# A gated attention and convolution block: first products stored unscaled, a second buffer for the attention's values, the gate pool opened after the attention

## The chip, the core and the metric

One core of a Trainium2 chip runs the whole layer in one launch. The metric is device microseconds of an execution; the median of three runs of the kernel before is 1504.21 us (1502.57 to 1506.20). The profiled execution took 1508.27 us, with a span of 1506.5 us from its first to its last instruction. Engines: PE multiplies matrices (PEld loads its weights), DVE and ACT work element by element, POOL and SP here mostly issue transfers (DMA). Each engine runs its own instructions in order and waits on semaphores of the others.

## The reference

x is 2048 tokens by 1024 in float32. Cut to what matters:

```python
h = rmsnorm(x, norm_g)
q, k, v, z_att, gb, gc, u, z_conv, g_att, g_conv = split(h @ w_in)       # 1024 x 6144
att = chunked_rel_attention(q, k, v, rel_bias)      # 8 heads of 64; own chunk of 64 and 8 to the left
y_att = (att * silu(z_att)) @ w_att_out
vconv = causal_depthwise_conv(gc * u, conv_w, conv_b)
y_conv = (gb * vconv * silu(z_conv)) @ w_conv_out
m = sigmoid(g_att) * y_att + sigmoid(g_conv) * y_conv
out = rmsnorm(x + m @ w_out, final_norm_g)
```

rmsnorm multiplies each token by r = 1/sqrt(mean(x^2) + eps), so that a product of unscaled x can be multiplied by r afterwards. The sigmoids are computed as 0.5 (1 + tanh(0.5 g)).

## The kernel before

**Precision and tiles.** Every large product is made of three fp32r passes: each operand is split into a high part (an ACT cast) and a low part (a DVE subtraction), and `passes` (L137) issues high x high, high x low and low x high for each of four blocks of 128, that is 12 matmuls of 128x128 by 128x512. The input projection works on tokens in two halves of 1024 and on weight columns in 24 pairs of two blocks of 128. For each pair and half it makes seven products instead of eight, numbered 1, 2, 6, 7, 4, 5, 3 (`ORDER`), of sums and differences of quarters: the operands of x are called t1 to t7 (`operand_steps`, each four tiles: t10h, t10l, t11h ...), those of the weights wc (`operand`, L377), which are also stored to HBM in the first half and loaded from there in the second. `seq` lists all products (pair, number) in order; before product s the weights of product s + 3 are made.

**The first products.** The first three pairs (`PLAIN`) of the first half are gate columns. They are done as twelve direct products of 24 matmuls each, on unscaled x, in the order (pair, 512 tokens, block) of `plain` (L642), while r (tiles rb, one for each 512 tokens) is worked out beside them. Each of the first four is copied out of PSUM by ACT and scaled later; of the others DVE reads PSUM itself and multiplies by rb (`scaled`, L652). Then ACT takes the Tanh and issues the store of the gate (`ev_gate`, L413). `between` builds t1, t2, t6, t7, t4 from the sixth product on. Products use three PSUM banks in turn (`ps_d`). In this stretch the order on PE, DVE and ACT is that of the code; elsewhere a scheduler orders all engines by its own estimate.

**Seam of the halves.** While the last pair of the first half runs, t1 to t7 of the second half are built, one set each time the list `due` says so (L849: two products after each of that pair's seven). The last pairs' results (silu of z, tiles sz; v) are evacuated at the same time.

**The attention** (`attention`, L145) runs between the products of the second half, spread evenly over them: 32 steps of (512 queries, head), four units each, and the values product (`att_v`, L229) three units behind. Its loads are issued by POOL: `load_qk` one head ahead, into two buffers, and `load_v` for the present head, into one buffer vv.

**The output stage.** For each half, `half_c` takes 16 items (branch i, 128 columns d) of two products each: wy times mid, then DVE combines with the gate tiles gl and so evacuates PSUM (L960, L963). Gates come from HBM through a pool gp of five tiles, which is opened some pairs before the attention ends (L867); `make_c` loads weights and gates one item ahead. `mix` prepares the operands of `half_d`, the last projection with the residual and the final norm.

Tiles named e(...) come from a pool of eight, used in turn, and slot(...) from one of 56. SP issues most of the other transfers, in one queue.

## Time and profile before

| what | us |
|---|---|
| median of three runs | 1504.21 |
| profiled execution / its span | 1508.27 / 1506.5 |
| PE busy / DVE / ACT / POOL | 1475.3 / 1090.5 / 740.1 / 163.8 |
| mean granted clock of PE | 0.995 |
| first products, from the first matmul on x | 8.3 to about 85.5 |
| second half begins | about 499 |
| output stage begins | 1172.0 |

In a row of the order of time the first number is the start in us, the second the length, and the bracket holds the idle time of that engine before it and what ended it. A row of the list of waits gives the total, the number and the longest. In the table of stretches each engine has its busy time and its number of instructions, and the three numbers at the end are the granted clock of PE (1.00 is full), the mean share of the DMA engines and the rate in GB/s. DMA is idle in much of the first products and near full from 90 us on.

### The profile page before, as it was taken

The page shows a single profiled execution, that of the slowest core. Times are in us where ns is not written, and L with a number is a line of the kernel's source. Part 1 is how long each engine was busy: PE and PEld are TensorE (multiplying, and loading weights), DVE is VectorE, ACT ScalarE, POOL GpSimd, SP SyncE. Part 2 cuts the span into 40 slices and gives each one's busy share as a digit, 9 for nine tenths or more (in the row PEclk, how much of TensorE's full clock was granted, in tenths as well). Part 3 has the DMA queues.
Part 4 walks back from the last instruction along what each step waited for, and adds up shares of the span by engine and source line. Part 5 has one row for each costly group of instructions (what it writes and reads, how often), then busy time and mean ns, then how long its engine had stood idle before and what let it go on. Part 6 is the DMA issues. An engine that isn't in the chain of part 4 may idle for free. (4 is left out here: it accounts for less than half of the span.)

```text
span 1506.5 us, 21077 instructions
## 1 busy us (share of the span) xinstructions
PE 1475.3 (98%) x6976; PEld 1226.2 (81%) x6976; DVE 1090.5 (72%) x2121; ACT 740.1 (49%) x1399; POOL 163.8 (11%) x310
## 2 busy tenths in 40 slices
PE   8899999999999999999999999999999999999997
PEld 6778888888877788887888888888888888888886
DVE  7977588596557784676677777787765577767687
ACT  7363453444345333565566666666666223423153
POOL 0000000000000002232222323322220000010000
PEclk9999999999999999999999999999999999999999
DMA  5279899989988895999898887878989845877443
GB/s 214 73 273 352 308 361 351 348 295 328 345 304 287 314 341 173 339 341 337 288 295 286 259 260 249 265 256 264 310 282 314 307 129 168 294 262 240 153 162 112
DMA packets 168748, 408.28 MB, mean 271 GB/s; under 512 B 21056, under 2 KB 41536, under 8 KB 168640
## 3 DMA queue, kind: packets, MB, share of 16 engines
q1 hardware_dynamic: 137008, 316.48, 60.7%
q0 software_dynamic: 22272, 73.42, 15.4%
q10 hardware_dynamic: 9360, 17.04, 3.1%
q8 instruction: 55, 0.90, 0.2%
q14 instruction: 53, 0.43, 0.1%
HBM read 251.67 MB, written 155.19 MB: 270 GB/s over the span
## 5 line engine op out<-in xcount | busy, mean ns | idle before, releaser
L162 POOL DMA_DIRECT2D q<-q x128 | 66.8, 527 | 675.5 <-DVE wc L128 585.0
L204 ACT ACTIVATE pr<-ps_s,nmax 128x640 f32<-128x640 f32 (+4 forms) x128 | 93.5, 730 | 93.0 <-DVE nmax L200 92.3
L206 ACT ACTIVATE pr<-pr,rs 128x640 f32<-128x640 f32 (+4 forms) x128 | 97.9, 765 | 35.3 <-DVE rs L205 34.9
L200 DVE CUSTOM_DVE_ANT_0 ps_s<-ps_s,bs 128x640 f32<-128x640 f32 (+4 forms) x128 | 95.3, 744 | 23.7 <-PE ps_s L194 22.4
L140 PE MATMUL ps_d<-mid,wy 128*128 128x512 f32 x256 | 99.7, 389 | 0.8 <-ACT wy L127 0.8
L128 DVE TENSOR_TENSOR wc<-wraw,wc 128x512 fp32r<-128x512 f32 x120 | 82.3, 688 | 24.7 <-ACT wc L127 24.5
L141 PE MATMUL ps_d<-mid,wy 128*128 128x512 f32 x256 | 99.6, 389 | 0.0
L194 PE MATMUL ps_s<-kk,q 128*128 128x320 f32 (+1 forms) x448 | 98.5, 334 | 1.0 <-ACT pr L204 0.5
L142 PE MATMUL ps_d<-mid,wy 128*128 128x512 f32 x256 | 99.3, 389 | 0.0
L220 DVE TENSOR_TENSOR pt<-ps_t,pt 128x640 fp32r<-128x640 f32 (+4 forms) x128 | 94.1, 735 | 3.4 <-ACT pt L219 2.5
L127 ACT CAST wc<-wraw 128x512 fp32r<-128x512 f32 x120 | 74.1, 621 | 44.2 <-PE ps_c L142 23.0
L219 ACT CAST pt<-ps_t 128x640 fp32r<-128x640 f32 (+4 forms) x128 | 80.1, 626 | 21.9 <-PE ps_t L214 20.7
L214 PE MATMUL ps_t<-ident,pr 128*128 128x128 f32 x560 | 82.3, 273 | 0.2
L229 PE MATMUL po<-pt,vv 128*128 128x512 f32 x336 | 75.5, 356 | 4.1 <-DMA vv<-v 3.2
L229 PEld LDWEIGHTS po<-pt,vv 128*128 128x128 f32 x336 | 62.1, 188 | 19.1 <-issue 3.5
L214 PEld LDWEIGHTS ps_t<-ident,pr 128*128 128x128 f32 x560 | 65.7, 140 | 9.9 <-issue 1.5
L194 PEld LDWEIGHTS ps_s<-kk,q 128*128 128x128 f32 x448 | 67.6, 190 | 5.6 <-ACT pr L204 4.8
L997 PE MATMUL ps_w<-wo,lefth 128*128 128x512 f32 (+1 forms) x240 | 71.9, 382 | 0.0
L140 PEld LDWEIGHTS ps_d<-mid,wy 128*128 128x128 f32 x256 | 48.0, 188 | 11.1 <-ACT wy L127 1.2
L234 DVE TENSOR_TENSOR ot<-po,ot 64x256 f32<-64x256 f32 x64 | 26.6, 415 | 41.3 <-ACT ot L233 40.4
L141 PEld LDWEIGHTS ps_d<-mid,wy 128*128 128x128 f32 x256 | 48.0, 188 | 10.1
L142 PEld LDWEIGHTS ps_d<-mid,wy 128*128 128x128 f32 x256 | 48.1, 188 | 9.9
(535 smaller groups left out, 4110.4 us busy)
## 6 DMA issues: line engine op xcount, KB each, us to landing
wc<-wc SPq DMA_DIRECT2D x294, 512.0 KB, 5.3
wraw<-wp_in SPq DMA_DIRECT2D x54, 512.0 KB, 5.8
q<-q POOLq DMA_DIRECT2D x128, 128.0 KB, 5.0
gl<-gate SPq DMA_DIRECT2D x64, 256.0 KB, 2.8
mid<-mid SPq DMA_DIRECT2D x64, 256.0 KB, 5.3
wor<-wo SPq DMA_DIRECT2D x56, 256.0 KB, 5.2
bs<-bias POOLq DMA_DIRECT2D x32, 320.0 KB, 7.7
v<-vst SPq DMA_DIRECT2D x64, 128.0 KB, 4.6
```

The costliest lines, as they stand in the source:

```text
L128: nc.vector.tensor_sub(w[:, 1], src, w[:, 0].bitcast(F32))
L140: nc.tensor.matmul(ps, lhsT=w[:, 0, k, :], rhs=rh[:, cs], start=(first and not onto and k == 0), stop=False, skip_group_check=onto)
L141: nc.tensor.matmul(ps, lhsT=w[:, 0, k, :], rhs=rl[:, cs], start=False, stop=False, skip_group_check=onto)
L142: nc.tensor.matmul(ps, lhsT=w[:, 1, k, :], rhs=rh[:, cs], start=False, stop=(last and k == len(rhs) - 1), skip_group_check=onto)
L194: nc.tensor.matmul(ps[:, i, :m], lhsT=q[s][:, g * P:(g + 1) * P], rhs=kk[:, k1 - n + i * m:k1 - n + (i + 1) * m], start=(s == 0), stop=(s ...
L200: nc.vector.tensor_tensor_reduce(out=view, in0=view, in1=bv, scale=-0.125, scalar=3.0e38, op0=ALU.add, op1=ALU.min, accum_out=nmax)
L204: nc.scalar.activation(out, view, AF.Exp, bias=nmax, scale=-1.0, accum_out=rs)
L206: nc.scalar.activation(pr[:, :n], pr[:, :n], AF.Identity, scale=rs)
L214: nc.tensor.transpose(out=ps[:, j * P:(j + 1) * P], in_=pr[:, j * P:(j + 1) * P], identity=ident)
L219: nc.scalar.copy(hi[:, js, qs], src)
L220: nc.vector.tensor_sub(lo[:, js, qs], src, hi[:, js, qs].bitcast(F32))
L229: nc.tensor.matmul(ps[:, :, a * P:b * P], lhsT=vv[:, g0 + j, :], rhs=pt[:, j, :, a * P:b * P], start=(i == 0), stop=(i == len(js) - 1))
```

## The change

- The twelve first products are all copied out of PSUM by ACT and stored as they are by SP (`plain_d`); the two rb tiles are stored too. `scaled` and the deferred Tanh are gone from this stage.
- In the output stage's first half the gates of the three unscaled columns are loaded, multiplied by rb (loaded again as `rbs`) on DVE and put through Tanh on ACT. The items' order begins with columns 3 and 7, which have no such gates, and `mix` follows it.
- vv gets two buffers and is loaded one head ahead, with q and k; the load of z stays where it was.
- gp is opened only when the attention is over; the first item's gates go into tiles of the pool of eight.
- The sets t1 to t7 of the second half are built at products 2, 3, 5, 8, 12, 15, 17 counted from the last pair's first (before: 2, 3, 4, 6, 8, 10, 12).

```diff
+TURN = (2, 3, 5, 8, 12, 15, 17)
...
+    plain_d = [dram.tile([P, CH], F32, name=f"plain{q}") for q in range(4 * PLAIN)]
+    rb_d = [dram.tile([P, CH], F32, name=f"rb{c}") for c in range(2)]
...
         def load_v(c, h):
-            vv = at([P, 8, P], "vv")
+            vv = at([P, 8, P], "vv", bufs=2)
...
+
+        def load_z(c, h):
             if h % 2 == 0:
...
         load_qk(*todo[0])
+        load_v(*todo[0])
...
                     load_qk(*todo[i // 4 + 1])
+                    load_v(*todo[i // 4 + 1])
                 elif i % 4 == 2:
-                    load_v(*todo[i // 4])
+                    load_z(*todo[i // 4])
...
-    def gate(i, d, c):
-        g = gp.tile([P, CH], F32, tag="g", name="gl")
-        nc.sync.dma_start(g, gate_d[i][d][c])
+    def gate(i, d, c, make):
+        g = make("gl")
+        nc.sync.dma_start(g, plain_d[plain.index((d, i, c))] if unscaled(d, c) else gate_d[i][d][c])
         return g
 
-    ITEMS_C = [(i, d) for dd in ((0, 4, 1, 5), (2, 6, 3, 7)) for i in (1, 0) for d in dd]
+    def unscaled(d, c):
+        return d < PLAIN and c < 2
+
+    ITEMS_C = [(i, d) for dd in ((3, 7, 0, 4), (1, 5, 2, 6)) for i in (1, 0) for d in dd]
...
-    def scaled(p, n, c, src):
-        t = src if src.space != PSUM else e("c")
-        nc.vector.tensor_mul(t, src, rb[c])
-        late.append(lambda: evs[p][n](c, c, t))
...
                 rb[0] = inverse(ry[0], e)
+                store(rb_d[0], rb[0])
...
-            if q < 4:
-                t = e("plain")
-                nc.scalar.copy(t, ps)
-                copied.append(lambda p=p, n=n, c=c, t=t: scaled(p, n, c, t))
-            else:
-                now, late = late, []
-                between(q)
-                if q > 4:
-                    scaled(*held0)
-                held0 = (p, n, c, ps)
-                for fn in now:
-                    fn()
+            t = e("plain")
+            nc.scalar.copy(t, ps)
+            store(plain_d[q], t)
+            between(q)
...
-            due.append(s + 2)
+                due = [s + d for d in TURN]
...
-        if n == NPAIR + 2 + PLAIN + 16 and i == 1:
-            conv_stack.close()
-            gp = pool("gp", 5)
         if n == 2 * NPAIR - 1 and i == 5:
-            made = make_c(0, ITEMS_C[0])
+            made = make_c(0, ITEMS_C[0], e)
+            rbs = [fslot("rbs") for c in range(2)]
+            for c in range(2):
+                nc.sync.dma_start(rbs[c], rb_d[c])
...
     banks.close()
+    conv_stack.close()
+    gp = pool("gp", 5)
...
+            if d < PLAIN and not hf:
+                for c in cs:
+                    nc.vector.tensor_mul(gl[c], gl[c], rbs[c])
+                    nc.scalar.activation(gl[c], gl[c], AF.Tanh, scale=0.5)
...
-                mix((7, 10, 14, 15).index(n_))
+                mix((3, 0, 1, 2)[(7, 10, 14, 15).index(n_)])
```

How the instructions move, at three places. First ACT among the first products, from the last cast of t6 on (c and plain are results on their way to a gate, wc the first weights of the seven-product part). Before:

```order
L133 CAST t63h<-xs 128x512
L416 ACTIVATE plain<-plain 128x512
L417 DMA gate_0_1_156<-plain 128x512
L416 ACTIVATE plain<-plain 128x512
L417 DMA gate_0_1_188<-plain 128x512
L416 ACTIVATE c<-c 128x512
L417 DMA gate_1_1_160<-c 128x512
L133 CAST t70h<-xs 128x512
L133 CAST t71h<-xs 128x512
L133 CAST t72h<-xs 128x512
L133 CAST t73h<-xs 128x512
L416 ACTIVATE c<-c 128x512
```

Now:

```order
L136 CAST t63h<-xs 128x512
L721 COPY plain<-ps_p 128x512
L136 CAST t70h<-xs 128x512
L136 CAST t71h<-xs 128x512
L136 CAST t72h<-xs 128x512
L136 CAST t73h<-xs 128x512
L721 COPY plain<-ps_p 128x512
L136 CAST t40h<-xs 128x512
L136 CAST t41h<-xs 128x512
L136 CAST t42h<-xs 128x512
L136 CAST t43h<-xs 128x512
L130 CAST wc<-wraw 128x512 x2
```

The Tanh and the gate's issue are gone, a copy out of PSUM stands between the sets, and the first wc is twelve rows behind t63h. Second, DVE at the seam of the halves (sz are silu values that SP stores as z, v and u results on their way, t71l to t50l splits for the second half). Before:

```order
L468 SCALAR_TENSOR_TENSOR sz<-sz,v 128x512
L134 TENSOR_TENSOR t40l<-xs,t40h 128x512
L358 TENSOR_TENSOR xs<-xs 128x512
L134 TENSOR_TENSOR t41l<-xs,t41h 128x512
L358 TENSOR_TENSOR xs<-xs 128x512
L134 TENSOR_TENSOR t42l<-xs,t42h 128x512
L815 TENSOR_TENSOR v<-v,ps_c 128x512
L134 TENSOR_TENSOR t43l<-xs,t43h 128x512
L362 TENSOR_TENSOR t_4851<-xs 128x512
L468 SCALAR_TENSOR_TENSOR sz<-sz,v 128x512
L468 SCALAR_TENSOR_TENSOR sz<-sz,ps_c 128x512
L134 TENSOR_TENSOR t50l<-t_4851,t50h 128x512
```

Now:

```order
L475 SCALAR_TENSOR_TENSOR sz<-sz,v 128x512
L137 TENSOR_TENSOR t72l<-xs,t72h 128x512
L809 TENSOR_TENSOR v<-v,ps_c 128x512
L137 TENSOR_TENSOR t73l<-xs,t73h 128x512
L365 TENSOR_TENSOR xs<-xs 128x512
L475 SCALAR_TENSOR_TENSOR sz<-sz,v 128x512
L475 SCALAR_TENSOR_TENSOR sz<-sz,ps_c 128x512 x2
L137 TENSOR_TENSOR t40l<-xs,t40h 128x512
L365 TENSOR_TENSOR xs<-xs 128x512
L137 TENSOR_TENSOR t41l<-xs,t41h 128x512
L137 TENSOR_TENSOR t42l<-xs,t42h 128x512
L137 TENSOR_TENSOR t43l<-xs,t43h 128x512
```

All sz now stand ahead of t40l; t5 follows further on. Third, POOL at the attention's second head. Before:

```order
L166 DMA kk<-k_0_109 128x512
L169 DMA bs<-bias_476 128x640
L177 DMA vv<-v_0_123 128x512
L182 DMA zs<-z_0_139 128x512
L162 DMA q_5884<-q_0_0_83 64x512 x2
L162 DMA q_5885<-q_1_0_87 64x512 x2
L166 DMA kk<-k_0_111 128x512
L169 DMA bs<-bias_477 128x640
L177 DMA vv<-v_0_125 128x512
```

Now:

```order
L169 DMA kk<-k_0_109 128x512
L172 DMA bs<-bias_490 128x640
L180 DMA vv<-v_0_125 128x512
L187 DMA zs<-z_0_139 128x512
L165 DMA q_5886<-q_0_0_83 64x512 x2
L165 DMA q_5887<-q_1_0_87 64x512 x2
L169 DMA kk<-k_0_111 128x512
L172 DMA bs<-bias_491 128x640
L180 DMA vv<-v_0_127 128x512
```

The values of head n + 1 (v_0_125 is the second head's) stand where those of head n stood. PE's own order differs by the place of one matmul on t20l, near 90 us, and of one in the output stage.

## The prediction

> **What bounds the kernel now.** I read the page's first part, then the waits of PE (the matmul engine), then the granted clock in short windows, and last the order of time on the engines around each wait.

> ```profile
> PE 1475.3 (98%) x6976; PEld 1226.2 (81%) x6976; DVE 1090.5 (72%) x2121; ACT 740.1 (49%) x1399; POOL 163.8 (11%) x310
> ```
> PE is busy for 1475.3 of 1506.5 us, so TensorE bounds the kernel and the change, which leaves the matmuls alone, can only win PE's idle time (31 us with the start and the end) and time at a lowered clock. The list of PE's waits (engine, line, releaser: total us, times, longest) says where:

> ```profile
> PE ps_p L140 <- DVE c L654: 4.7, 2, 2.9
> PE ps_c L140 <- ACT wc L127: 4.4, 2, 3.2
> PE po L229 <- DMA vv<-v: 3.2, 2, 1.8
> PE ps_d L140 <- ACT t33h L133: 1.8, 1, 1.8
> PE ps_d L140 <- ACT wc L127: 1.1, 1, 1.1
> PE ps_d L140 <- DMA wc<-wc: 0.9, 1, 0.9
> PE po L229 <- DVE w L825: 0.8, 1, 0.8
> PE ps_d L140 <- ACT wy L127: 0.8, 1, 0.8
> ```
> In order of time on PE, start and length first, the wait in brackets:

> ```profile
> 22.29 0.40 PE L141 MATMUL ps_p<-rawl,w 128*128 128x512 f32 x1
> 32.73 0.39 PE L142 MATMUL ps_p<-rawh,w 128*128 128x512 f32 x1
> 58.66 0.66 PE L140 MATMUL ps_p<-rawh,w 128*128 128x512 f32 x1 [1.86 <-DVE c L654]
> 74.27 0.50 PE L140 MATMUL ps_p<-rawh,w 128*128 128x512 f32 x1 [2.87 <-DVE c L654]
> 88.65 0.50 PE L140 MATMUL ps_c<-t10h,wc 128*128 128x512 f32 x1 [3.16 <-ACT wc L127]
> 720.03 0.59 PE L229 MATMUL po<-pt,vv 128*128 128x512 f32 x2 [1.84 <-DMA vv<-v]
> 1159.32 1.39 PE L229 MATMUL po<-pt,vv 128*128 128x512 f32 x6 [0.82 <-DVE w L825]
> ```
> The granted clock (PE busy, clock, DMA share and rate; two-us windows):

> ```profile
> 58.00:60.00 2.00, 1.34 (x4) 0.70 0.00 0
> 60.00:62.00 2.00, 2.00 (x6) 0.50 0.94 256
> 74.00:76.00 2.00, 1.73 (x8) 1.00 0.69 259
> 90.00:92.00 2.00, 2.00 (x6) 0.50 1.05 178
> ```
> and, with all engines in five-us windows, around the wait at 720:

> ```profile
> 720.00:725.00 5.00, 4.97 (x18) 4.26 (x19) 2.47 (x6) 2.05 (x5) 0.00 (x0) 0.66 0.97 333
> ```
> A wait of 1.84 us was followed by a window at 0.66, which is 5 x 0.34 = 1.7 us more; the wait before 58.66 by 0.6 + 1.0 = 1.6 us; the longer one before 74.27 by nothing.

> **Part 1, the first products.** The twelve plain products keep their matmuls. What goes is each product's multiplication by rb (L654, DVE), its Tanh and its store on ACT; what comes is one ACT copy each (four had one) and a store on SP, and PSUM is freed by that copy. The end of this stage is set by ACT and DVE, which must split the operands t1, t2, t6, t7, t4 before ACT reaches the first wc:

> ```profile
> 65.77 0.62 ACT L133 CAST t60h<-xs 128x512 fp32r<-128x512 f32 x1 [5.05 <-DVE xs L356]
> 72.27 0.62 ACT L133 CAST t63h<-xs 128x512 fp32r<-128x512 f32 x1 [1.90 <-DVE xs L356]
> 75.88 0.62 ACT L133 CAST t70h<-xs 128x512 fp32r<-128x512 f32 x1 [0.40 <-ACT c L416]
> 80.32 0.62 ACT L133 CAST t40h<-xs 128x512 fp32r<-128x512 f32 x1 [1.73 <-DVE xs L358]
> 86.44 0.62 ACT L133 CAST t43h<-xs 128x512 fp32r<-128x512 f32 x1 [1.42 <-DVE xs L358]
> 87.98 1.14 ACT L127 CAST wc<-wraw 128x512 fp32r<-128x512 f32 x2 [0.40 <-ACT c L416]
> ```
> I redo this chain in the new order on ACT. Two casts start 1.14 - 0.62 = 0.52 us apart. The two PE rows at 22.29 and 32.73 are 46 matmuls apart: 0.227 us each, 5.45 us for a product of 24. On DVE, seven L654 multiplications (some 0.6 us each, counted in its order) ahead of t6 are gone, 4.2 us, so ACT is what is late. (1) t60h now stands behind the copy of the ninth product. That product needs no DVE any more: it starts at 58.66 - 1.86 = 56.80 and ends at 62.25, the copy takes 0.52, t60h comes at 62.8 for 65.77. (2) t60h to t63h is the same add, cast, subtract chain, 6.5 us; I add 0.5, because in it stands an add on weights whose fetch now starts later (SP sends it behind the eighth store): t63h at 69.8. (3) Between t63h and t70h stood three Tanh with their issues, 3.61 us; now cast and copy, 1.04: t70h at 70.8. (4) From t70h to t40h 4.44 us, less one L654: 3.8, t40h at 74.6. (5) t40h to t43h unchanged, 6.12: 80.7. (6) A Tanh and its issue stood before wc; now it is 0.52 behind: 81.2, and the matmul follows 0.67 after the cast as now (87.98 to 88.65): 81.9. **Gain: 88.65 - 81.9 = 6.8 us.** The product phase itself ends at 56.80 + 4 x 5.45 = 78.6, so a wait of some 3.3 us stays, with its spell at clock 0.50 as at 90. The low clock after 58.66 goes too, but wins nothing of its own, as PE was waiting anyway. Bounds: 88.65 - 78.6 = 10.0 above; nothing below, where the stream behind eats it (rival A). Behind SP's twelve stores are the wraw, x and wc transfers, in the order they had; each store waits only for a copy that PE's next step needs anyway.

> **Part 2, the values.** POOL's queue (issue times, what it waited for):

> ```profile
> 696.59 0.55 POOL L177 DMA_DIRECT2D vv<-v  x1 [9.29 <-PE ps_t L214]
> 711.39 0.55 POOL L177 DMA_DIRECT2D vv<-v  x1 [2.05 <-PE ps_t L214]
> 1151.03 0.55 POOL L175 DMA_DIRECT2D vv<-v  x1 [8.95 <-PE po L229]
> ```
> The single buffer comes free when the last head's product is done, and the matmul at 720.03 waited 8.6 us behind the issue. The row at 1159.32 names DVE w, but comes 8.3 us behind its issue in the same way; I count it as the same wait. With two buffers the queue waits at the same places, for the head before, but what it fetches there is needed one head later, about 15 us (696.59 to 711.39). All three waits go: 3.2 + 0.8 = 4.0, and with them the low clock at 720, 1.7. **Gain: 5.7 us.** Bounds 3.2 (only what DMA is named for) and 6.5 (1159 with a low clock as well). Behind the waiting fetch stand z and the next q, k and bias, which waited behind it before too.
> [...]

> **Part 3, the seam of the halves.** TURN builds t6, t7, t4, t5 and t3 of the second half 1, 2, 4, 5 and 5 products later. DVE has no gap there, and SP's queue stands behind it:

> ```profile
> 497.67 0.44 SPq L383 DMA_DIRECT2D wc<-wc  x1
> 502.68 0.32 SPq L474 DMA_DIRECT2D z<-sz  x1
> 505.02 0.62 SPq L383 DMA_DIRECT2D wc<-wc  x1
> ```
> The last z values come out of DVE here, start first:

> ```profile
> 502.56 0.69 DVE L468 SCALAR_TENSOR_TENSOR sz<-sz,ps_c 128x512 f32<-128x512 f32 x1
> 506.16 0.69 DVE L468 SCALAR_TENSOR_TENSOR sz<-sz,ps_c 128x512 f32<-128x512 f32 x1
> ```
> Each z store holds up the wc loads behind it, and PE waits 0.9 and 1.8 us (wc, and the one put down to t33h). In the new order of DVE the last sz stands eleven instructions earlier: 6.6 us at 0.6. The load at 505.02 can go some 4 us earlier, more than the 1.8. **Gain: 2.7 us**, bounds 0 (another row of that queue holds it) and 3.2 (with the 0.5 us wait on v). The moved splits are still six products, 16 us, ahead of use. The two waits of 1.1 and 1.2 us on wc (4.4 in the list, less the 3.2 at 88) are outside it and stay.

> **Part 4, the output stage.** It gets 12 multiplications (0.6 us) on DVE, 12 Tanh (0.5) on ACT, and gates that are fetched only when the attention is over. Cover:

> ```profile
> gl<-gate SPq DMA_DIRECT2D x64, 256.0 KB, 2.8
> 1175.00:1200.00 25.00, 25.00 (x112) 20.71 (x111) 12.48 (x20) 4.58 (x8) 0.00 (x0) 1.00 0.89 302
> 1200.00:1225.00 25.00, 25.00 (x112) 20.67 (x112) 20.54 (x34) 7.38 (x13) 0.00 (x0) 1.00 0.65 206
> ```
> DVE has 17 us free in these 50, ACT 38. A gate takes 2.8 us to land and about 1.3 to scale, 4.1 together; an item is two products, 5.45 us, and its gates are asked for an item ahead. With three PSUM banks an evacuation may come 5 us late before PE waits. I take 0; bounds +0.8 (the wait on wy at the stage's start goes) and -7 (rival B).

> **Sum.** 6.8 + 5.7 + 2.7 = 15.2 us. The profiled execution took 1508.27, which lies 4.1 above the median of the runs, 1504.21; it would take 1493.1. From the median: **1489.0 us**.

> **Rivals.** *A: the stage behind the first products takes the gain back.* The DMA engines run full there from 90 us (share 1.05 above), x of the second half and the stores of wc in one stream:

> ```profile
> 114.74 0.69 DVE L392 TENSOR_TENSOR s<-wraw 128x512 f32<-128x512 f32 x1 [1.75 <-DMA wraw<-wp_in]
> 128.66 0.69 DVE L392 TENSOR_TENSOR s<-wraw 128x512 f32<-128x512 f32 x1 [3.19 <-DMA wraw<-wp_in]
> ```
> If these waits grow by what the start is earlier, and reach PE, 6.8 us are lost: 1495.8. Against it: the bytes come in the same order, only earlier, and PE never waited there. *B: the first gates come late.* In the new order DVE scales item 2's gates ahead of item 1's evacuation; if they land later than an evacuation can slip, PE waits up to an item, 5.45, plus 1.7 of low clock: 1496.2. *C: slower.* Every scaled item (six in the first half of this stage) waits for its whole chain of 4.1 us, because five buffers are too few to fetch ahead: 24.6 us, 1513.6. It decides from 15.2 / 6 = 2.5 us an item. Against it: each buffer is free again at least an item and a half before its next use. *D: the change doesn't do what it says,* all three waits having a second cause just behind: 1504. *E: the low clock stays.* The 1.84 us before 720.03 did not lower the clock, something else in the windows before did, and 1.7 us at 0.66 remain somewhere in the attention: 1490.7. Against it: the wait of 1.86 us before 58.66 was followed by the same.

> **How the numbers follow.** Forecast 0.57 (its own range 1485 to 1493), A 0.15, B 0.12, C 0.05, D 0.06, E 0.05. The range goes down to 1484.5 (the upper bounds of parts 1 and 2 in part) and up past A and B to 1499.5. A difference under 0.2%, 3 us, can't be told from none here. Forecast, A, B and E are beyond it: 0.89, of which I keep 0.87, since A and B could come together; within it D and that, 0.08; slower C, 0.05.

> **What would show it.** First matmul on wc at 81 to 83 us for 88.65, no wait on ps_p; no wait on vv, no low clock near 720; none over 1 us around 500; PE full from the output stage's start. I am wrong if PE waits on wc between 85 and 130, or on gl's evacuation after the attention.

## The result, and the profile after

The change makes the kernel faster by about 8 us, where 15 were forecast. Beside each other on one chip the kernel before had a median of 1504.37 us (1502.57 to 1506.20) and the changed one of 1496.14 us (1494.30 to 1498.76). The ratio is 0.9945 with a 95% interval of 0.9929 to 0.9961, which is 5.9 to 10.7 us. The profiled execution of the change took 1497.31 us (span 1495.5), 11.0 us less than the profiled one of before.

PE is busy for the same share of the span as before, and the list of its waits (engine, line, releaser: total us, times, longest) is of another make:

```profile
PE 1472.5 (98%) x6976; PEld 1223.9 (82%) x6976; DVE 1090.9 (73%) x2121; ACT 746.2 (50%) x1407; POOL 163.8 (11%) x310
```

```profile
PE ps_c L143 <- ACT wc L130: 3.8, 2, 2.5
...
PE po L234 <- DVE pt L225: 1.6, 2, 0.8
PE ps_d L143 <- DMA wc<-wc: 1.4, 1, 1.4
...
PE ps_d L143 <- ACT wc L130: 1.1, 1, 1.1
PE ps_t L219 <- DVE pt L225: 1.0, 2, 0.8
PE ps_s L199 <- ACT pr L209: 0.9, 1, 0.9
PE ps_d L143 <- ACT wy L130: 0.8, 1, 0.8
...
PE ps_d L143 <- ACT gl L945: 0.3, 1, 0.3
```

The waits of ps_p on DVE and the waits on vv and on t33h are gone. Those on pt and pr are 3.5 us together, where the list before had only 0.5 us on pr. In order of time on PE:

```profile
81.27 0.50 PE L143 MATMUL ps_c<-t10h,wc 128*128 128x512 f32 x1 [2.52 <-ACT wc L130]
...
668.48 1.10 PE L234 MATMUL po<-pt,vv 128*128 128x512 f32 x4 [0.80 <-DVE pt L225]
698.84 1.08 PE L234 MATMUL po<-pt,vv 128*128 128x512 f32 x4 [0.76 <-DVE pt L225]
951.70 0.77 PE L219 MATMUL ps_t<-ident,pr 128*128 128x128 f32 x5 [0.79 <-DVE pt L225]
953.41 1.03 PE L199 MATMUL ps_s<-kk,q 128*128 128x320 f32 x4 [0.95 <-ACT pr L209]
```

Both executions have the same 6976 matmuls in nearly the same order, so their starts can be set against each other, the first with the first and so on. The start in the changed kernel less the start before gives a running account of where the time went (each column is rounded by itself):

| place in the program | after minus before, us | this step |
|---|---|---|
| first matmul on wc (88.65, now 81.27) | -7.4 | -7.4 |
| some four us later (low clock there before, none now) | -9.0 | -1.6 |
| before the seam of the halves (484 us) | -9.0 | 0 |
| behind the seam (511, now 499 us) | -11.4 | -2.4 |
| attention, behind the old waits on vv and their low clock (725 us before) | -14.7 | -3.4 |
| attention, at 958 us now | -11.6 | +3.1 |
| end of the attention (1148 us now) | -12.2 | -0.6 |
| first gates of the output stage (1205 us now) | -11.1 | +1.1 |
| end | -11.0 | +0.1 |

The row with +3.1 is the loss that the prediction did not have: 1.6 of it comes by 954 us, most of that from the waits at 951 to 953 (1.7 us, where the kernel before has 0.5), and 1.5 from a spell at half clock behind them (3.41 us from 953.9). This is DVE there, start and length first, the idle time before it and its releaser in brackets:

```profile
950.50 0.41 DVE L240 TENSOR_TENSOR o<-po,ot 64x256 f32<-64x256 f32 x1 [2.61 <-DMA mid<-o]
950.84 0.81 DVE L225 TENSOR_TENSOR pt<-ps_t,pt 128x640 fp32r<-128x640 f32 x1
```

and POOL, which issued that store:

```profile
945.43 0.57 POOL L248 DMA_DIRECT2D mid<-o  x1
```

o is the attention's result of a pair of heads, and has one buffer. DVE may not write the next pair's first result into it before the store of the last pair has been read out of it, 4.5 us after the issue at 946.0. Behind this instruction in DVE's order stands the low part of pt, and PE waits for that. Over the whole attention, the group of these instructions:

```profile
L240 DVE TENSOR_TENSOR o<-po,ot x64: 403/417/420, 604.8 to 1157.4; 64x256 f32<-64x256 f32 x64
...
  DMA mid<-o: 8.8, 5
```

DVE sat 8.8 us at five such places, 4.4 in the kernel before. At the place of the +3.1 the kernel before has the same wait. There its store was read out 3.2 us after the issue, and PE waited 0.5 us behind it:

```profile
960.00 0.56 POOL L243 DMA_DIRECT2D mid<-o  x1
963.72 0.42 DVE L235 TENSOR_TENSOR o<-po,ot 64x256 f32<-64x256 f32 x1 [1.11 <-DMA mid<-o]
```

### The profile page after: what moved, and what is told of

The parts are those of the page before. It is cut to its first block, busy times and chain, and to the rows that moved or that the text cites. A ratio compares the mean times of both kernels' runs of the same rounds, so it can differ in the third digit from the quotient of the medians.

```text
span 1495.5 us, 21091 instructions
## 1 busy us (share of the span) xinstructions
PE 1472.5 (98%) x6976; PEld 1223.9 (82%) x6976; DVE 1090.9 (73%) x2121; ACT 746.2 (50%) x1407; POOL 163.8 (11%) x310
## 5 line engine op out<-in xcount | busy, mean ns | idle before, releaser
L899 ACT ACTIVATE wo<-wor 128x512 fp32r<-128x512 f32 x56 | 34.5, 629 | 60.1 <-DMA wor<-wo 53.1
L143 PEld LDWEIGHTS ps_d<-mid,wy 128*128 128x128 f32 x256 | 48.0, 188 | 12.2 <-ACT wy L130 1.5
## 6 DMA issues: line engine op xcount, KB each, us to landing
mid<-mid SPq DMA_DIRECT2D x64, 256.0 KB, 5.6
wor<-wo SPq DMA_DIRECT2D x56, 256.0 KB, 5.0
gl<-gate SPq DMA_DIRECT2D x52, 256.0 KB, 3.1
```

What stands on the lines that cost most here:

```text
L143: nc.tensor.matmul(ps, lhsT=w[:, 0, k, :], rhs=rh[:, cs], start=(first and not onto and k == 0), stop=False, skip_group_check=onto)
```

## The experiments

The kernels were run in three groups on three chips. In each group the kernel before was timed beside them: its medians were 1506.35, 1506.33 and 1504.73 us, so across groups the ratios to it are compared. The last column is the profiled execution's span.

| run | median us | ratio to before, 95% | span us |
|---|---|---|---|
| scaled first products (part 1 undone) | 1503.35 | 0.9989 (0.9977 to 1.0002) | 1499.5 |
| one values buffer (part 2 undone) | 1498.44 | 0.9954 (0.9942 to 0.9967) | 1495.5 |
| old turn (part 3 undone) | 1497.13 | 0.9950 (0.9933 to 0.9967) | 1493.4 |
| two buffers for o | 1495.57 | 0.9937 (0.9924 to 0.9949) | 1493.1 |
| the change again | 1499.26 | 0.9953 (0.9934 to 0.9971) | 1497.0 |
| two buffers for o, spaced | 1494.56 | 0.9917 (0.9901 to 0.9934) | 1491.4 |
| and sums first | 1487.57 | 0.9873 (0.9853 to 0.9893) | 1485.9 |
| no scaling in the output stage | 1495.59 | 0.9927 (0.9907 to 0.9946) | 1493.1 |
| kernel before, again | 1504.58 | one run | 1502.8 |
| sums first, one values buffer | 1490.99 | 0.9917 (0.9902 to 0.9932) | 1488.5 |
| sums first, old turn | 1491.51 | 0.9911 (0.9899 to 0.9924) | 1488.4 |
| sums first, other space | 1491.22 | one run | 1489.5 |

**Part 1 undone.** The first products are as in the kernel before, and the output stage scales nothing; all else is the change.

```diff
-            t = e("plain")
-            nc.scalar.copy(t, ps)
-            store(plain_d[q], t)
-            between(q)
+            if q < 4:
+                t = e("plain")
+                nc.scalar.copy(t, ps)
+                copied.append(lambda p=p, n=n, c=c, t=t: scaled(p, n, c, t))
+            else:
+                now, late = late, []
...
```

> The changed kernel with part 1 alone undone: the first twelve products are scaled, sent through Tanh and stored as finished gates at once, as before; the output stage scales nothing. Theory (the sum of three parts): PE's first matmul on wc goes back from 81.3 to 88.6 us and a half-clock spell of 3.41 us follows its wait, 7.4 + 1.6 = 9.0 us lost; the output stage wins back the 1.2 us it lost; 1496.1 + 7.8 = 1503.9. Rival (the stage behind the first products holds PE anyway): at most 3 us are lost, 1499.

The two late matmuls come back to the hundredth of a us:

```profile
74.26 0.50 PE L141 MATMUL ps_p<-rawh,w 128*128 128x512 f32 x1 [4.37 <-DVE c L662]
88.65 0.50 PE L141 MATMUL ps_c<-t10h,wc 128*128 128x512 f32 x1 [1.64 <-ACT wc L128]
```

Against the profile of the change the run is 7.4 us behind from here to 668 us, so the stage behind the first products takes nothing back, and the rival falls. A half-clock spell came behind the first of the two waits (matmuls 0.43 us apart from 75.15 to 78.14 us, 0.23 from 78.47 on), where PE had to wait again anyway, and none behind the second, so 7.4 and not 9.0 were lost here. At the end only 4.1 us are left: 1.7 us of the waits on pt (668 and 699 us) do not come in this execution, others behind o cost 0.8 more, no spell at half clock follows them (1.5), and 0.9 is won where the output stage no longer scales. The median is 4.1 us above that of the change run again (1499.26), with nearly equal medians of the kernel before; by the ratios, 0.9989 against 0.9945 and 0.9953, part 1 is worth 5.4 to 6.6 us.

**Part 2 undone.**

```diff
-            vv = at([P, 8, P], "vv", bufs=2)
+            vv = at([P, 8, P], "vv")
...
-                    load_v(*todo[i // 4 + 1])
                 elif i % 4 == 2:
+                    load_v(*todo[i // 4])
                     load_z(*todo[i // 4])
```

> The changed kernel with part 2 alone undone: one buffer for the values, loaded at its own head. Theory (a new wait took most of the gain: DVE waits to overwrite o until the store of o has landed, and PE waits for DVE's pt): the waits on vv come back (two of 1.4 to 1.8 us and the one of 0.8 at 1159), the waits on pt at 668, 699 and 951 get shorter, and the net loss is 1 to 2 us: 1497 to 1498. Rival (the buffer alone was worth what was forecast): 5.7 us lost, 1501.8.

The ratio, 0.9954, is that of the change, 0.9945 and 0.9953. The waits on vv did not come back either, except for one of 0.84 us on po at 677 us, put down to a DVE instruction, and DVE waited 6.0 us for the store of o where it had waited 8.8. The longest wait of this run in the attention is a third thing, on DVE and then on PE:

```profile
1134.85 1.36 DVE L943 TENSOR_TENSOR gl<-gl,rbs 128x512 f32<-128x512 f32 x2 [3.52 <-DMA rbs<-rb]
```

```profile
1137.74 1.65 PE L234 MATMUL po<-pt,vv 128*128 128x512 f32 x6 [2.24 <-DVE pt L225]
```

The scheduler put the first multiplication of a gate by rbs, part 4 of the change, into DVE's order before the attention was over, and its transfer had not landed. In the change itself the same multiplication stands behind the attention, at 1170 us. Between 1100 and 1148 us this run loses 4.1 us on the change for it, a spell at half clock included. So it can't price the buffer: with a cost that the change doesn't have it is as fast as the change. What it does show is that one buffer alone need not bring 4 us of waits on vv.

**Part 3 undone.**

```diff
-TURN = (2, 3, 5, 8, 12, 15, 17)
+TURN = (2, 3, 4, 6, 8, 10, 12)
```

> The changed kernel with part 3 alone undone: the operands of the second half are built at products 2, 3, 4, 6, 8, 10, 12. Theory: waits of 0.9 us on wc and of 1.8 us on t33h come back around 500 us, the 1.4 us on wc that the changed kernel has there goes: 1 to 2.4 us lost, 1497.3 to 1498.5. Rival (the seam's gain came from the earlier start, not from the order): the time stays at 1496.1.

The profile shows the loss where it was expected, the medians do not. The wait on t33h is there:

```profile
PE ps_d L143 <- ACT t33h L136: 2.7, 1, 2.7
```

From 484 to 504 us the run loses 2.4 us on the change, in three steps of 0.6, 0.5 and 1.3. The name t33h is a coincidence of times. The matmul reads t20h and wc, and it starts at 503.60 us, 0.13 us after a wc load has landed; in the kernel before it starts at 510.84, again 0.13 us after a wc load, and in that kernel's second profile (below) it starts ahead of the cast of t33h, 0.14 us after the load. So this is a wait on a wc load, as the prediction had it. Between 660 and 958 us the run gains 5.0: its waits on pt and pr are 2.9 us shorter, and no half clock follows them. So neither theory is settled by this run; the waits behind o had to go first.

**Two buffers for o.** To make room for the second one, two scratch vectors went from three buffers to one; this frees 128 bytes of SBUF per partition.

```diff
-        a = small.tile([P, n], F32, name="ra", tag="ra")
-        q = small.tile([P, n], F32, name="rq", tag="rq")
+        a = small.tile([P, n], F32, name="ra", tag="ra", bufs=1)
+        q = small.tile([P, n], F32, name="rq", tag="rq", bufs=1)
...
-                pair[c, h // 2] = (zs, at([P, CH], "o", F32))
+                pair[c, h // 2] = (zs, at([P, CH], "o", F32, bufs=2))
```

> The changed kernel with two buffers instead of one for o, the attention's result of a head pair (two scratch vectors of the norm go to one buffer to make room). Theory: DVE's five waits for the store of o (8.8 us in all) go, and with them PE's waits on pt and pr at 664, 668, 699 and 951 to 953: 0.2 + 0.8 + 0.8 + 0.8 + 0.9 = 3.5 us, and up to 1.7 more where a half-clock spell followed: 1492.6, down to 1490.9. Rival (DVE and ACT are late there for another cause, the store only hides it): PE waits as before, 1496.

The mechanism is as the theory says: DVE never waits for the store of o, and PE's list has neither pt nor pr. By the end of the attention the run is 5.4 us ahead of the profile of the change, of the 5.2 expected. But at the end it is only 2.4 ahead, with no wait to show for it. The windows of 40 us show that PE was full at full clock and still did less (PE busy with its matmuls, PEld, DVE, ACT, POOL, the clock, DMA share and rate). First the change, then this run:

```profile
1260.00:1300.00 40.00, 40.00 (x178) 33.14 (x177) 33.12 (x60) 24.19 (x49) 0.00 (x0) 1.00 0.70 237
```

```profile
1260.00:1300.00 40.00, 40.00 (x174) 32.46 (x174) 32.58 (x60) 20.31 (x42) 1.83 (x4) 1.00 0.74 250
```

Between 1250 and 1300 us a matmul starts every 0.2267 us in the change and every 0.2312 us here, about a quarter of them 0.237 to 0.241 us behind the last. These are the matmuls of the last product, which take their weights and their moving operand from two pools, op at the far end of SBUF and tt at the near end. The 128 bytes that were freed lie below tt and not below op: the distance between the two pools, modulo 2048 bytes, went from 512 to 640. (A tile of tt and each half of a tile of op take 2048 bytes of a partition, so all tiles of a pool share one remainder: in the programs as built it is 2016 for op in both, and for tt 1504 in the change and 1376 here.)

**The change again, spacing, sums first, and no scaling.** The change itself was run once more beside three others.

> The changed kernel once more, for the comparison on one chip. Theory (the waits on pt at 668, 699 and 951 are not the same in every execution, since they hang on when the store of o lands): 1496 to 1498, and the profile shows other waits on pt than the first, or none at 668 and 699. Rival (they belong to the program): 0.8 us at 668, 0.8 at 699 and 1.7 at 951 again.

```profile
PE ps_d L143 <- DMA wc<-wc: 1.8, 1, 1.8
PE ps_t L219 <- DVE pt L225: 1.7, 1, 1.7
...
PE ps_s L199 <- ACT pr L209: 0.9, 1, 0.9
...
PE po L234 <- DVE pt L225: 0.8, 1, 0.8
```

The wait at 668 us is gone, the one near 700 is there again, and the ones at 951 to 953 are longer (1.7 and 0.9). The sum is 3.4 us, as it was 3.5. That the sums agree says little: in the profiles with the same attention and one buffer for o they are 0.6 us (old turn) and 1.8 us (no scaling, below). So the places belong to the program, while what each costs changes from one execution to the next.

```diff
+    pool("pad", side="right").tile([P, 32], F32, name="pad")
     op = pool("op", 12, side="right")
```

> Two buffers for o as before, with 128 bytes left free ahead of the output stage's pool, so that the distance in SBUF between the operands of its matmuls is again what it was (it had changed by the 128 bytes that made room). Theory (the distance slowed the matmuls): between 1250 and 1470 us one every 0.2267 us again and not 0.231, 3.0 us less than with two buffers alone: 1492.6. Rival (the slower matmuls have another cause): 1495.6 again.

```profile
1260.00:1300.00 40.00, 40.00 (x179) 33.10 (x177) 32.95 (x61) 20.62 (x43) 1.69 (x4) 1.00 0.72 245
```

The matmuls run at 0.2267 us again, and the ratio falls from 0.9937 to 0.9917, 3.0 us of 1505. The intervals of the two overlap, but the profiles say the same: from 1205 us to the end, two buffers alone lose 2.6 us on the change, and the spaced ones nothing. Nothing but the place of one pool was changed. Against the change in the same group (0.9953) the second buffer of o is worth 0.0036, 5.4 us, though the intervals just touch (0.9934); the profiles say 5.6 us.

```diff
+            def sums_first(j):
                 if i == 6:
                     nc.vector.tensor_add(b11[:, j, :], b11[:, j, :], b12[:, j, :])
                 elif i == 4:
                     nc.vector.tensor_sub(b21[:, j, :], b21[:, j, :], b11[:, j, :])
+            if not half:
+                for j in range(4):
+                    sums_first(j)
+            for j in range(4):
+                if half:
+                    sums_first(j)
...
                 split_t(half, i, j, t1 if i == 5 else src[:, j, :])
```

> The same, and in the first half the four sums that t6 and the four that t4 need are each put ahead of the four splits on DVE, so that ACT need not wait for each sum in turn. Theory (the chain of casts sets PE's first matmul on wc): t43h is cast about 4 us earlier than at 80.1 us, PE's wait of 2.5 us before 81.3 goes, as far as the end of the products at 78.7, and with it the half-clock spell that follows it in some runs: 2.5 to 4.2 us less than without it, 1489 to 1490. Rival (the next thing is late there, the weights' wc or the x behind it): under 1 us.

```profile
64.43 0.62 ACT L136 CAST t63h<-xs 128x512 fp32r<-128x512 f32 x1
...
75.35 0.62 ACT L136 CAST t43h<-xs 128x512 fp32r<-128x512 f32 x1
75.88 1.14 ACT L130 CAST wc<-wraw 128x512 fp32r<-128x512 f32 x2
```

t43h is cast at 75.35 us instead of 80.08, PE goes from the first products to wc without a wait (its matmul at 78.5 us), and no half clock follows (the matmuls stay 0.23 us apart). The median is 1487.57 us: 7.0 us less than without it, more than the 2.5 to 4.2 of the theory; the profiled spans differ by 5.5 us. Of these 4.6 are there by 90 us, start and clock together, 0.4 come at the seam and 0.5 at the first gates. What the rest of the 7.0 is stays open; four runs are few. This kernel beats both others: its ratio of 0.9873 (0.9853 to 0.9893) to the kernel before is 19 us.

```diff
             if d < PLAIN and not hf:
                 for c in cs:
-                    nc.vector.tensor_mul(gl[c], gl[c], rbs[c])
-                    nc.scalar.activation(gl[c], gl[c], AF.Tanh, scale=0.5)
+                    pass
```

> The changed kernel with the twelve multiplications by rb and the twelve Tanh in the output stage left out, so those gates are wrong. Theory (they delay the evacuations there): the 0.3 us wait on gl at 1204.5 and the other small ones between 1160 and 1205 go, 1.2 us less. Rival (the gates' loads, not their scaling, are late; or nothing): the time stays within 0.3 us.

The wait on gl is gone, and from 958 us to the end this run gains 1.0 us on the change's first profile, of the 1.2 expected. The gates are loaded as before here, so the wait hung on their scaling, not on their loads alone. The ratio, 0.9927 against 0.9953, has an interval too wide to say more.

**The third group.** The kernel before once more, unchanged:

> The kernel before, profiled once more. Theory (the waits on vv are not the same in every execution, as those on pt were not): its 1.4 us at 688 and 1.8 us at 720 are gone or of another size, and other waits behind the store of o stand in their place; the waits of the first products (1.9, 2.9 and 3.2 us) are the same. Rival: all the waits are as in the first profile.

```profile
PE po L229 <- DMA vv<-v: 2.2, 3, 1.2
```

```profile
686.71 0.59 PE L229 MATMUL po<-pt,vv 128*128 128x512 f32 x2 [1.20 <-DMA vv<-v]
...
960.34 0.42 DVE L235 TENSOR_TENSOR o<-po,ot 64x256 f32<-64x256 f32 x1 [2.07 <-DMA mid<-o]
963.26 0.86 PE L194 MATMUL ps_s<-kk,q 128*128 128x320 f32 x4 [0.95 <-ACT pr L204]
```

The waits of the first products are the same (2.7 and 3.2 us the longest), those on vv are 2.2 us in place of 3.2. At 717 us PE waited 0.5 us for vv where it had waited 1.84, and no low clock followed (1.00 between 720 and 725 us, where the first profile has 0.66): of the 3.7 us by which this span is shorter, 2.8 lie there. The first profile had shown a dear execution of that wait.

The last two lines show that the wait for the store of o costs the kernel before time as well, 1.2 us of PE at this place. The eight profiles with one buffer for o can be lined up here. The store landed 3.06 us after its issue (kernel before), 3.06 (old turn), 3.09 (one values buffer), 3.67 (no scaling), 4.02 (kernel before, again), 4.41 (the change), 4.71 (scaled first) and 5.34 (the change again), and PE lost 0.45, 0.64, 0.52, 1.01, 1.21, 1.74, 2.05 and 2.67 us. In the six profiles with two buffers for o it landed after 3.4 to 6.1 us, and PE lost nothing. So the loss at this place was not made by the change: it is there in both kernels, and it grows with the time that one store takes to land.

Then part 2 and part 3 undone in the fastest version, with the same edits as above:

> The fastest version (two buffers for o, spacing kept, sums first) with one buffer for the values, loaded at its own head: part 2 of the change undone where the store of o no longer covers it. Theory (part 2 is worth little on its own): under 1.5 us more, 1487.6 to 1489, with waits on vv of 1 us in all at most. Rival (the store of o hid its worth): the waits on vv of 3.2 us and the one of 0.8 come back, 4.0 to 5.7 us more, 1491.6 to 1493.3.

```profile
PE po L234 <- DMA vv<-v: 0.8, 2, 0.6
```

The waits on vv are 0.8 us, as the theory had it. The price is not settled: the profiles differ by 2.6 us, 0.6 of it ahead of the second half (0.4 at the seam, on a wc load) and 2.0 in the attention; the medians by 3.4 (1490.99 to 1487.57); the ratios by 0.0044, which is 6.6 us, with intervals that do not meet. The fastest version was not run in this group, so that something of the chip may be in the 6.6. With o out of the way the second values buffer is worth more than nothing, 2 us where the profiles can place it. Two of the six runs took 1494 us, the others 1490 to 1491, so this price varies too.

> The fastest version with the old products for the second half's operands: part 3 undone where the waits behind o can't blur it. Theory: 2.4 us more, 1490.0, with a wait of over 2 us on t33h around 500. Rival (the times of the undisturbed comparison, which showed no loss): under 1 us more.

```profile
497.33 0.47 PE L143 MATMUL ps_d<-t20h,wc 128*128 128x512 f32 x1 [2.13 <-DMA wc<-wc]
```

Here there is a loss: 3.9 us by the medians, 5.7 by the ratios (0.9911 to 0.9873, again across groups), 2.5 by the profiles' ends. At the seam itself it is 3.4 us. PE waits 2.1 us on a wc load, where the fastest version waits 1.1, and 0.8 us more on v before it; a spell at half clock (matmuls 0.43 us apart from 497.94 to 500.93 us), which the fastest version does not have there, costs the other 1.6. So without the spell part 3 is worth some 1.8 us here, by a wc load, as its working had it.

> The fastest version with 256 bytes instead of 128 left free ahead of the output stage's pool: the distance between its matmuls' operands is then 384 bytes (modulo 2048), where 512 ran at 0.2267 us a matmul and 640 at 0.231. Theory (any distance that is no multiple of 512 slows them): 0.229 to 0.231 us between 1250 and 1300, 3 us more. Rival (only distances above 512 do): 0.2267 us.

```profile
1260.00:1300.00 40.00, 40.00 (x174) 32.40 (x174) 31.28 (x64) 18.66 (x38) 2.17 (x4) 1.00 0.81 279
```

At a distance of 384 the matmuls take 0.2314 us, as at 640, and the run ends 3.6 us behind the fastest version's profile, 0.7 of it by a wait on a gate tile. Of the three distances tried between these two pools only 512 ran at 0.2267 us.

## Why the prediction was right or wrong

**What bounds the kernel**: right. All that the change won or lost was PE's idle time and its clock: of the 11.0 us between the two spans 8.2 are idle time of PE (31.2 us before, 23.0 now) and 2.8 its busy time (1475.3 and 1472.5), with one spell at half clock between 20 and 1400 us where there were three.

**Part 1** (6.8): right, step by step. These are the casts that were foretold at 62.8, 69.8, 70.8, 74.6, 80.7 and 81.2 us:

```profile
62.95 0.62 ACT L136 CAST t60h<-xs 128x512 fp32r<-128x512 f32 x1
69.35 0.62 ACT L136 CAST t63h<-xs 128x512 fp32r<-128x512 f32 x1 [1.36 <-DVE xs L363]
70.35 0.62 ACT L136 CAST t70h<-xs 128x512 fp32r<-128x512 f32 x1
74.14 0.62 ACT L136 CAST t40h<-xs 128x512 fp32r<-128x512 f32 x1 [0.16 <-DVE xs L365]
80.08 0.62 ACT L136 CAST t43h<-xs 128x512 fp32r<-128x512 f32 x1 [1.36 <-DVE xs L365]
80.60 1.14 ACT L130 CAST wc<-wraw 128x512 fp32r<-128x512 f32 x2
```

No step is off by more than 0.7 us, and the matmul came at 81.27 for 81.9: 7.4 us for 6.8. The extra 0.5 for a later weight fetch was not needed. That the spell at half clock stays was wrong in the first profile (1.6 us more were won) and right in the second; it is there in five of the seven profiles that have this part and not yet the sums first. Rival A did not happen: the account stays at -9.0 from 93 to 484 us.

**Part 2** (5.7): the removal is right, the gain is not. The waits on vv, the one at 1159 us and the low clock at 720 are gone, as foretold. The step that failed is "All three waits go: 3.2 + 0.8 = 4.0, and with them the low clock at 720, 1.7". It takes one execution's waits for the program's: those on vv are 2.2 us and without a low clock in the kernel before's second profile, and 0.8 in the fastest version with one values buffer. And it has no term for the other single buffer of the same stretch, o. The waits behind its store were 0.5 us in the profile that was read; in the change's they are 3.5, with 1.5 of low clock behind them.

How much of this is the program and how much the execution can be read from the time that each profile spends between the seam and the end of the attention. The five profiles with two buffers for both o and v lie within 0.2 us of one another there. Against these, the profiles with two values buffers and one for o lose 0.7 us (old turn), 2.1 (no scaling), 3.1 (scaled first), 5.7 and 5.3 (the change, twice), and the kernel before loses 6.5 and 3.8 in its two. So the store of o takes something in every one of them, and that it takes most in the change's own two is chance, as far as the other three with the same attention show. The means, 5.2 before and 3.4 with the second values buffer, leave some 2 us for part 2, from few profiles. Whether the earlier loads of vv make the stores of o land later is not shown. Among the rivals D came nearest, a second cause just behind the first, but it was priced for all parts together and had no name.

**Part 3** (2.7): the cause is right, a wc load held up in SP's queue, and the size nearly. The account says 2.4, and 1.4 when the kernel before's second profile is taken; the run that undoes it in the fastest version says 1.8 and a spell. Wrong is "none over 1 us around 500": 1.4 us on wc at 499 stay, from the same queue.

**Part 4** (0): mis-sized. The first gates land late, as rival B had it, but cost about 1.0 to 1.2 us and not 5.45: DVE waits 5.2 us in all for them, the evacuations behind their scaling slip, and PE waited 0.3 at 1204.5 and small amounts before. The two runs without the scaling won 0.9 and 1.0 us there. The 0.8 us on wy at the stage's start stayed.

**The sum**: 15.2 forecast, 11.0 between the two profiles, 8.2 between the medians. Of the 4.2 between 15.2 and 11.0, part 1 gave 2.2 more, the attention 4.8 less (the table's -3.4, +3.1 and -0.6 make 0.9 of 5.7), part 3 0.3 less and part 4 1.2 less. The 2.8 between 11.0 and 8.2 are the two profiled executions' own places among their runs: 3.9 us above the median before, 1.2 above it after. The prediction took a gain that it had read in a dear execution off the median, although part of that gain, the long waits on vv and the spell at 720, was what made the execution dear: 2.8 of the 3.7 us by which the second profile is shorter lie there.

That the measured 1496.14 lies inside the range is luck. It is outside the forecast's own range, 1485 to 1493, and inside the whole one, which reached up for rivals A (1495.8) and B (1496.2). A did not happen, and B cost 1.2 us at most.

**Rival E** (the low clock has another cause) is not borne out as it was put, but it touched the point that matters, which follows.

## What the runs showed of the hardware

```profile
80.00:85.00 5.00, 3.73 (x16) 2.97 (x17) 4.28 (x8) 3.86 (x8) 0.00 (x0) 1.00 0.48 148
```

In the second, 2.72 of 2.79 us fell into one window:

```profile
80.00:85.00 5.00, 3.85 (x10) 3.09 (x11) 4.36 (x8) 3.66 (x7) 0.00 (x0) 0.66 0.51 157
```

A spell cost up to 1.7 us here, half of its 3.41 (1.7 at 720 us before, 1.5 at 953.9 in the change), and nothing of its own where PE had to wait again anyway (behind 74.26 in the run with scaled first products). One program therefore differs from execution to execution by the spells it catches, and a price read from one profile with a spell in it has up to 1.7 us of luck in it.

**The rate of the matmuls went with a distance in SBUF.** It was 0.2267 us at 512 bytes (modulo 2048) between the pools of the two operands (the change; two buffers for o, spaced), 0.2312 at 640 (two buffers for o) and 0.2314 at 384 (sums first, other space), with PE full, no wait shown and the full clock. These are means between 1250 and 1300 us. As the programs place their tiles, 384 matmuls of the last product have one operand in each of the two pools; they take 0.2330 us at 640 and 0.2331 at 384. The others, whose operands lie a multiple of 2048 bytes apart, keep their rate within 0.001 us in both. Neither pool's own place explains it: op lies where it lay in the change when the matmuls slow down (remainder 2016), and tt lies the same when they recover (1376). It cost 3.0 us by the ratios, 2.6 by the profiles, in a stage of some 250 us. What makes the distance matter was not shown.

## What to carry to other kernels

When a buffer is doubled to remove a wait, list the other single buffers that the same engines cross in that stretch, and ask what each costs when its store or load lands late: the store of o cost PE between 0.45 and 2.67 us at one place, by how late it landed. Profile the kernel twice before a wait on a transfer is priced, and take a gain off the time of the execution in which it was read. Count a half-clock spell behind a wait as luck, unless 2.1 us or more of the wait fell into one window of the grid: here all ten such windows were followed by a spell, and of those with 1.74 to 1.87 us five in seven. Where a chain of sum, cast and subtraction passes to and fro between two engines, try writing all the sums first, which took t43h's cast here from 80.08 to 75.35 us; and after any change in how much SBUF the early pools take, compare the matmul rate of every stage, not only the waits: 0.2267 us became 0.2312 here with no wait to show for it.
